# Modulation sums in PSUM banks, closed half a group later

## The chip, the cores and the metric

One core of one Trainium2 chip runs the whole program. The metric is the device time in microseconds (us) of one execution, as a median over several. The engines are PE (TensorE matmul), DVE (VectorE), ACT (ScalarE), POOL (GpSimd) and SP (SyncE, whose queue issues nearly all DMAs here).

## What is computed

A residual stream of 512 tokens by 1024 features, in fp32, goes through two blocks of two layers each. Block 1 has two hybrid layers, each with two attentions and then a squared-relu MLP with 4096 hidden features. Block 2 (an MLA layer and a gated linear attention layer, each with such an MLP) also has a context stream of 256 tokens, and scales and shifts its norms by a modulation vector that does not depend on the tokens:

```python
def modulate(h, shift, scale):
    return h * (1.0 + scale) + shift

def sqrelu_mlp(h, w1, w2):
    return jnp.square(jax.nn.relu(h @ w1)) @ w2
...
    silu_c = jax.nn.silu(c)
    silu_cc = jax.nn.silu(c_ctx)
    for i in range(DEPTH):
        m_lat = (silu_c @ ada_w[i] + ada_b[i]).reshape(B, N_MOD, 1, D)
        m_ctx = (silu_cc @ ada_w[i] + ada_b[i]).reshape(N_MOD, D)
        h_lat = modulate(rms_norm_2(x_lat, norm_g[i, 0]), m_lat[:, 0], m_lat[:, 1])
```

For each layer of block 2 the modulation is thus two vector-matrix products, one for each stream, with the same weight of 1024 by 6144 fp32 (24 MB). The second layer needs only the first 2048 features of the context's vector. These vector-matrix products are what the change is about.

## The kernel before

**Products.** A product of two fp32 operands is made as three products of rounded parts (`mac3`): high by high (L211), low weight by high (L212), high weight by low (L213). Weights come in blocks of 512 KB on the SP queue (L185); ACT rounds them (L190, `wh`), and POOL subtracts to get the remainder (L194, `wl`), reading two SBUF tiles.

**The MLP.** `mlp` runs 8 chunks of 512 hidden features. `first(c+1)` makes 4 groups of 24 matmuls of 512 columns into the PSUM pool `mm` (2 banks), whose results DVE and ACT square and split (L522, L525, L529, L530). `second(c)` makes 8 groups of 12 matmuls, in turn into `mm` and `sp` (pool tag `s`, 4 banks), and DVE adds each to `y` in SBUF (L541). A chunk is 192 matmuls. A third PSUM pool, `tp`, has 2 banks, and serves transposes and small products.

**The modulation in the background.** While the MLP of layer l of block 1 runs, the generator `ada(l)` makes the modulation of layer l of block 2. `mlp` advances it by a step at fixed places: twice ahead of each of the two weight blocks of `first`, and three times (`BG = 3`) ahead of `second`, seven steps a chunk. A group u is 512 of the 6144 features, and takes four steps q. In each step a block `araw` of 2 x 128 rows by 512 features (512 KB, two buffers, SP queue, L1342) is loaded ahead, and DVE multiplies its rows, a row on a partition, with silu(c) of those rows and adds them to an accumulator of 128 partitions by 512, one accumulator for each stream:

```python
if q == 0 and k == 0:
    nc.vector.tensor_scalar(a, raw[:, k], sc, None, op0=ALU.mult)
else:
    nc.vector.scalar_tensor_tensor(a, raw[:, k], sc, a, op0=ALU.mult, op1=ALU.add)
```

That is L1370 and L1372: 16 instructions a group with two streams, 8 with one (layer 1 from u = 4 on). The accumulators (`aacc`) are SBUF tiles, two buffers. The sum over the 128 partitions closes a group, at the start of the first step of the next group: `total` splits an accumulator into a rounded part (ACT, L165) and the rest (DVE, L166) in tiles of the shared pool `tmp`, and PE multiplies both with a column of ones (L1351, L1352) into a bank of `tp`; ACT copies the row (L1354) and SP stores it (L1355).

**Order.** The program is written in this order; a scheduler then orders the instructions of each engine, and each engine runs its own list strictly in order. What an instruction on PE waits for, all matmuls behind it wait for too. The same holds for DVE, on which the accumulations, the splits and the evictions L522 to L541 share one list.

## Time and profile before

| | |
|---|---|
| median of 3 runs | 3557.34 us (3553.0, 3557.34, 3562.2) |
| the profiled execution | span 3557.3 us, nothing outside it that the views show |
| busy, share of the span | PE 93%, PE weight load 80%, DVE 64%, ACT 43%, POOL 33% |
| MLPs with the modulation in the background | from about 450 to 940 us and from about 1390 to 1860 us |
| MLP of the last layer, one stream, nothing in the background | from about 3230 us on |

In the views, PE is the matmul pipeline, "L1352" is line 1352 of the kernel shown above, and an arrow gives what released a wait. A matmul of 512 columns starts every 0.233 us at full clock although its record lasts 0.39 us, since matmuls overlap.

### The profile page before, as it was taken

Reading aid. Unit: us, or ns where it says so; the run is one execution under the profiler, and the core shown is the slowest. Engines: PE = TensorE matmul, PEld = TensorE weight load, DVE = VectorE, ACT = ScalarE, POOL = GpSimd, SP = SyncE. Lnnn points to the kernel's source line nnn. Section 1 sums busy time; section 2 is a strip of 40 time slices with the busy share of each in tenths; the row PEclk is TensorE's granted clock in tenths of the full one; section 3 lists DMA queues with packets and bytes.
Section 4 is the critical chain, followed back from the end, with each engine's and each line's share of the span. In section 5 each row is a group of like instructions: output and inputs, shape, how many; then the busy total and the mean of one; then the engine's idle time right before and its main releaser. Section 6 shows DMA issues by size and latency. Waiting matters only on the chain.

```text
span 3557.3 us, 49004 instructions
## 1 busy us (share of the span) xinstructions
PE 3299.7 (93%) x18723; PEld 2843.9 (80%) x18723; DVE 2263.8 (64%) x4044; ACT 1516.0 (43%) x3323; POOL 1191.2 (33%) x688
## 2 busy tenths in 40 slices
PE   8899988988989998989999999999999899889998
PEld 8788776766878887767778888888888788878887
DVE  6755668887686567886657763723433866873445
ACT  5455543222454454432235654531221456654223
POOL 3333334333333324334431332132232222124443
PEclk8999999999999999999999999999999999999999
DMA  5212444444232235345321113122122212123332
GB/s 171 66 60 75 166 140 152 135 145 131 82 92 72 74 114 177 116 158 176 119 74 59 37 60 97 48 63 68 60 64 63 69 53 66 63 70 95 95 95 77
DMA packets 262097, 337.68 MB, mean 95 GB/s; under 512 B 17107, under 2 KB 178110, under 8 KB 261734
## 3 DMA queue, kind: packets, MB, share of 16 engines
q1 hardware_dynamic: 261862, 334.55, 29.9%
q8 instruction: 147, 2.41, 0.3%
q14 instruction: 88, 0.72, 0.1%
HBM read 305.98 MB, written 28.52 MB: 94 GB/s over the span
## 4 chain that ended last, share of the span: by engine, by line
PE 62%; DVE 22%; ACT 8%; issue 5%; DMA 2%; POOL 1%; SPq 0%; DVEq 0%; ACTq 0%; POOLq 0%
PE mm L211 13%; PE mm L213 13%; PE mm L212 13%; PE s L212 4%; PE s L211 4%; PE s L213 4%; DVE aacc L1372 3%; ACT wh L190 2%; PE s L280 2%; DMA araw<-in_ada_w_dram 2%; DVE t L166 1%; PE tp L1065 1%; DVE t L529 1%; DVE wl L194 1%; PE mm L238 1%
## 5 line engine op out<-in xcount | busy, mean ns | idle before, releaser
L194 POOL TENSOR_TENSOR wl<-wraw,wh 128x1024 fp32r<-128x1024 f32 (+2 forms) x424 | 1008.4, 2397 | 1848.4 <-ACT wh L190 1800.2
L211 PE MATMUL mm<-h,wh 128*128 128x512 f32 (+1 forms) x1916 | 728.4, 380 | 30.1 <-ACT h L1264 8.5
L213 PE MATMUL mm<-h,wh 128*128 128x512 f32 (+1 forms) x1916 | 713.6, 373 | 6.0 <-DVE h L333 3.0
L212 PE MATMUL mm<-h,wl 128*128 128x512 f32 (+1 forms) x1916 | 716.4, 374 | 2.0 <-POOL wl L194 1.6
L190 ACT CAST wh<-wraw 128x1024 fp32r<-128x1024 f32 (+3 forms) x454 | 428.4, 967 | 512.1 <-issue 328.7
L211 PEld LDWEIGHTS mm<-h,wh 128*128 128x128 f32 x1916 | 370.2, 193 | 93.1 <-ACT h L1264 10.3
L213 PEld LDWEIGHTS mm<-h,wh 128*128 128x128 f32 x1916 | 369.1, 193 | 71.6 <-DVE h L1265 4.8
L212 PEld LDWEIGHTS mm<-h,wl 128*128 128x128 f32 x1916 | 371.0, 194 | 54.8 <-POOL wl L194 2.4
L529 DVE TENSOR_TENSOR t<-t 128x512 f32<-128x512 f32 (+1 forms) x140 | 169.2, 1208 | 256.3 <-ACT hid L525 256.0
L1372 DVE SCALAR_TENSOR_TENSOR aacc<-araw,sc,aacc 128x512 f32<-128x512 f32 x280 | 295.3, 1079 | 43.8 <-DMA araw<-in_ada_w_dram 41.8
L211 PE MATMUL mm<-hid,wh 128*128 128x512 f32 (+1 forms) x848 | 294.2, 347 | 9.7 <-DVE y L541 9.7
L212 PE MATMUL mm<-hid,wl 128*128 128x512 f32 (+1 forms) x848 | 292.4, 345 | 0.0
L213 PE MATMUL mm<-hid,wh 128*128 128x512 f32 (+1 forms) x848 | 291.3, 344 | 0.0
L541 DVE TENSOR_TENSOR y<-y,mm 128x512 f32<-128x512 f32 (+1 forms) x192 | 105.4, 549 | 201.7 <-PE mm L213 201.5
L211 PE MATMUL s<-hid,wh 128*128 128x512 f32 (+1 forms) x560 | 211.5, 378 | 0.0
L213 PE MATMUL s<-hid,wh 128*128 128x512 f32 (+1 forms) x560 | 211.4, 377 | 0.0
L212 PE MATMUL s<-hid,wl 128*128 128x512 f32 (+1 forms) x560 | 211.2, 377 | 0.0
L530 DVE TENSOR_TENSOR hid<-t,hid 128x512 fp32r<-128x512 f32 (+1 forms) x176 | 180.5, 1029 | 29.8 <-ACT t L527 25.4
L525 ACT ACTIVATE hid<-t 128x512 fp32r<-128x512 f32 (+1 forms) x176 | 97.2, 554 | 231.3 <-DVE t L522 155.6
L211 PEld LDWEIGHTS mm<-hid,wh 128*128 128x128 f32 x848 | 160.7, 190 | 33.0 <-DVE y L541 6.8
L213 PEld LDWEIGHTS mm<-hid,wh 128*128 128x128 f32 x848 | 160.7, 190 | 21.2
L212 PEld LDWEIGHTS mm<-hid,wl 128*128 128x128 f32 x848 | 160.7, 190 | 21.1 <-issue 0.3
(682 smaller groups left out, 7438.1 us busy)
## 6 DMA issues: line engine op xcount, KB each, us to landing
wraw<-in_w_ff_dram SPq DMA_DIRECT2D x128, 512.0 KB
wraw<-in_mlp_w_dram SPq DMA_DIRECT2D x128, 512.0 KB
araw<-in_ada_w_dram SPq DMA_DIRECT2D x96, 512.0 KB
wraw<-in_w_in_dram SPq DMA_DIRECT2D x68, 512.0 KB
raw<-in_cmp_w_dram SPq DMA_DIRECT2D x16, 512.0 KB
td<-t SPq DMA_DIRECT2D x32, 256.0 KB
h<-td SPq DMA_DIRECT2D x32, 256.0 KB
wraw<-in_w_out_dram SPq DMA_DIRECT2D x16, 512.0 KB
```

Source lines behind the costliest of these rows:

```text
L166: self.nc.vector.tensor_tensor(l, x, h.bitcast(F32), op=ALU.subtract)
L190: i = nc.scalar.copy(h[:, x:z], raw[:, x - a:z - a]).ins
L194: e.tensor_tensor(l[:, x:z], raw[:, x - a:z - a], h[:, x:z].bitcast(F32), op=ALU.subtract)
L211: nc.tensor.matmul(ps, wh, mh, start=first, stop=False)
L212: nc.tensor.matmul(ps, wl, mh, start=False, stop=False)
L213: nc.tensor.matmul(ps, wh, ml, start=False, stop=last)
L280: self.nc.tensor.matmul(ps, self.ones, acc, start=first, stop=last)
L525: nc.scalar.activation(h, a, AF.Square)
L529: nc.vector.tensor_tensor(a, a, a, op=ALU.mult)
L530: nc.vector.tensor_tensor(lo, a, h.bitcast(F32), op=ALU.subtract)
L541: nc.vector.tensor_tensor(y, y, ps, op=ALU.add)
L1372: nc.vector.scalar_tensor_tensor(a, raw[:, k], sc, a, op0=ALU.mult, op1=ALU.add)
```

## The change

The accumulators of `ada` are now PSUM tiles, one bank each, that take both banks of `tp`. The multiply-adds (now L1379 and L1381) read `araw` from SBUF and read and write the bank. A group's split (`part`) still stands at the start of the next group's first step, but goes into tiles of its own, `ada0` and `ada1`, with two buffers each in layer 0 and one in layer 1. For the four groups of layer 1 with two streams there is no split: ACT copies each accumulator in fp32 and one fp32 ones-product takes the copy. The ones-products (now L1363), the row copy (L1365) and the store (L1366) come at the third step of the next group, into a bank of `sp`. A step is added at the end. In `load_ctx` the transposes of the context, which run beside `ada(1)`, take banks of `sp` in place of `tp`. All other lines of the diff only drop comments and docstrings.

```diff
-        def total(u, acc):
-            for s, a in enumerate(acc):
-                h = self.t(self.tmp, [P, 512], F32R, tag="t")
-                lo = self.t(self.tmp, [P, 512], F32R, tag="t")
-                self.split(a, h, lo)
-                ps = self.ps(pool=self.tp, tag="tp")
-                nc.tensor.matmul(ps[0:1], self.onesr[:, 0:1], h, start=True, stop=False)
-                nc.tensor.matmul(ps[0:1], self.onesr[:, 0:1], lo, start=False, stop=True)
+        def part(acc):
+
+            nb = 2 if l == 0 else 1
+            if l and len(acc) == 2:
+                out = [[self.t(pool, [P, 512], F32, tag=f"ada{q}", bufs=nb)] for q in range(2)]
+                for a, (c,) in zip(acc, out):
+                    nc.scalar.copy(c, a)
+                return out
+            out = [[self.t(pool, [P, 512], F32R, tag=f"ada{q}", bufs=nb) for q in range(2)] for _ in acc]
+            for a, hl in zip(acc, out):
+                self.split(a, *hl)
+            return out
+
+        def total(u, parts):
+            for s, ms in enumerate(parts):
+                ps = self.ps(pool=self.sp, tag="s")
+                one = (self.ones if len(ms) == 1 else self.onesr)[:, 0:1]
+                for q, m in enumerate(ms):
+                    nc.tensor.matmul(ps[0:1], one, m, start=q == 0, stop=q == len(ms) - 1)
                 row = self.t(self.tmp, [1, 512], F32, tag="t")
                 nc.scalar.copy(row, ps[0:1])
                 nc.sync.dma_start(md[s, 4 * u:4 * u + 4].rearrange("a p -> (a p)")[None, :], row)
 
         nxt, done = load(0, 0), None
         for u in range(12):
-            if done:
-                total(*done)
-            acc = [self.t(pool, [P, 512], F32, tag="aacc", bufs=2) for _ in range(1 if l == 1 and u >= 4 else 2)]
+            acc = [self.ps(pool=self.tp, tag="tp") for _ in range(1 if l == 1 and u >= 4 else 2)]
             for q in range(4):
                 raw = nxt
                 if (u, q) != (11, 3):
@@ -1370,8 +1379,11 @@
                             nc.vector.tensor_scalar(a, raw[:, k], sc, None, op0=ALU.mult)
                         else:
                             nc.vector.scalar_tensor_tensor(a, raw[:, k], sc, a, op0=ALU.mult, op1=ALU.add)
+                if q == 2 and done:
+                    total(*done)
                 yield
-            done = u, acc
+            done = u, part(acc)
+        yield
         total(*done)
         yield
...
             for k in range(0, KT, 2):
                 if k == 4:
                     xt = load(1)
-                ps = self.ps(pool=self.tp, tag="tp")
+                ps = self.ps(pool=self.sp, tag="s")
                 for kk in range(2):
```

**PE, layer 0, the ones-products that close group u = 4.** Before, the list of PE has them one by one inside groups of `first`: `t_6409` and `t_6410` are the two parts of one stream's sum, `t_6419` and `t_6420` those of the other.

```order
L213 MATMUL mm_6453<-h_4609,wh_6443 128x512
L211 MATMUL mm_6453<-h_4638,wh_6443 128x512
L1351 MATMUL tp_6413<-t_6409,onesr_642 1x512
L212 MATMUL mm_6453<-h_4638,wl_6444 128x512
L213 MATMUL mm_6453<-h_4639,wh_6443 128x512
L211 MATMUL mm_6453<-h_4664,wh_6443 128x512
L1352 MATMUL tp_6413<-t_6410,onesr_642 1x512
L212 MATMUL mm_6453<-h_4664,wl_6444 128x512
L213 MATMUL mm_6453<-h_4665,wh_6443 128x512
```

After, the four stand together between a group of `first` and one of `second` (`ada_6409` and `ada_6410` are the same two parts as before).

```order
L212 MATMUL mm_6471<-h_4740,wl_6432 128x512
L213 MATMUL mm_6471<-h_4741,wh_6431 128x512
L1363 MATMUL s_6507<-ada_1196_6409,onesr_642 1x512
L1363 MATMUL s_6507<-ada_1197_6410,onesr_642 1x512
L1363 MATMUL s_6513<-ada_1198_6411,onesr_642 1x512
L1363 MATMUL s_6513<-ada_1199_6412,onesr_642 1x512
L211 MATMUL mm_6551<-hid_1111_5953,wh_6541 128x512
L212 MATMUL mm_6551<-hid_1111_5953,wl_6542 128x512
```

Each pair has moved from the middle of a group of 24 products to the end of a later one. In the whole list of before, 12 to 30 matmuls stand between the last matmul whose result DVE evicts ahead of a split and the L1352 that takes the split, for 33 of the 40 splits; after the change it is at least 52 for each of the 32 splits.

**DVE, layer 0, the splits of the same group.** Before, the splits L166 stand between the evictions L522 to L530 of `first`, and the first accumulations of the next group go around them.

```order
L522 SCALAR_TENSOR_TENSOR t_6374<-mm_6349,r_94 128x512
L529 TENSOR_TENSOR t_6374<-t_6374 128x512
L530 TENSOR_TENSOR hid_1179_6320<-t_6374,hid_1178_6319 128x512
L522 SCALAR_TENSOR_TENSOR t_6404<-mm_6379,r_94 128x512
L529 TENSOR_TENSOR t_6404<-t_6404 128x512
L166 TENSOR_TENSOR t_6410<-aacc_6173,t_6409 128x512
L530 TENSOR_TENSOR hid_1181_6322<-t_6404,hid_1180_6321 128x512
L1370 TENSOR_SCALAR aacc_6429<-araw_6333,sc_718 128x512
L1372 SCALAR_TENSOR_TENSOR aacc_6429<-araw_6333,sc_718,aacc_6429 128x512
L166 TENSOR_TENSOR t_6420<-aacc_6174,t_6419 128x512
```

After, both stand in a row ahead of that chunk's first L522.

```order
L541 TENSOR_TENSOR y_4754<-y_4754,mm_6279 128x512
L541 TENSOR_TENSOR y_4754<-y_4754,s_6293 128x512
L166 TENSOR_TENSOR ada_1197_6410<-tp_6161,ada_1196_6409 128x512
L166 TENSOR_TENSOR ada_1199_6412<-tp_6162,ada_1198_6411 128x512
L1379 TENSOR_SCALAR tp_6417<-araw_6333,sc_718 128x512
L1379 TENSOR_SCALAR tp_6418<-araw_6333,sc_718 128x512
L1381 SCALAR_TENSOR_TENSOR tp_6417<-araw_6333,sc_718,tp_6417 128x512
L1381 SCALAR_TENSOR_TENSOR tp_6418<-araw_6333,sc_718,tp_6418 128x512
L522 SCALAR_TENSOR_TENSOR t_6374<-mm_6349,r_94 128x512
```

The eviction of `mm_6349` has moved from ahead of both splits to behind them and behind four accumulations.

**DVE, layer 0, the end of the norm ahead of the MLP.** L260 and L287 to L289 end the norm that the MLP's first products need (`acc` and `ry` hold a sum of squares and its inverse root), L299 adds squares, `araw` are blocks of the modulation weight. Before:

```order
L1372 SCALAR_TENSOR_TENSOR aacc_5208<-araw_5236,sc_718,aacc_5208 128x512
L1372 SCALAR_TENSOR_TENSOR aacc_5209<-araw_5236,sc_718,aacc_5209 128x512
L299 TENSOR_TENSOR acc_95<-acc_95,t_4944 128x256
L299 TENSOR_TENSOR acc_95<-acc_95,t_4973 128x256
L299 TENSOR_TENSOR acc_95<-acc_95,t_5002 128x256
L299 TENSOR_TENSOR acc_95<-acc_95,t_5031 128x256
L260 TENSOR_SCALAR acc_95<-s_5093 128x256
L194 TENSOR_TENSOR wl_5223<-wraw_5224,wh_5222 128x512
L287 TENSOR_TENSOR ry_5098<-ry_5092 128x256
```

After:

```order
L1381 SCALAR_TENSOR_TENSOR tp_5603<-araw_5605,sc_718,tp_5603 128x512
L1381 SCALAR_TENSOR_TENSOR tp_5604<-araw_5605,sc_718,tp_5604 128x512
L1381 SCALAR_TENSOR_TENSOR tp_5603<-araw_5605,sc_718,tp_5603 128x512
L299 TENSOR_TENSOR acc_95<-acc_95,t_5031 128x256
L1381 SCALAR_TENSOR_TENSOR tp_5604<-araw_5605,sc_718,tp_5604 128x512
L1381 SCALAR_TENSOR_TENSOR tp_5603<-araw_5611,sc_718,tp_5603 128x512
L1381 SCALAR_TENSOR_TENSOR tp_5604<-araw_5611,sc_718,tp_5604 128x512
L1381 SCALAR_TENSOR_TENSOR tp_5603<-araw_5611,sc_718,tp_5603 128x512
L1381 SCALAR_TENSOR_TENSOR tp_5604<-araw_5611,sc_718,tp_5604 128x512
L1381 SCALAR_TENSOR_TENSOR tp_5603<-araw_5687,sc_718,tp_5603 128x512
L1381 SCALAR_TENSOR_TENSOR tp_5604<-araw_5687,sc_718,tp_5604 128x512
L260 TENSOR_SCALAR acc_95<-s_5093 128x256
```

Ten multiply-adds on three more blocks of weight (`araw_5605`, `araw_5611`, `araw_5687`, of group u = 1) now stand ahead of L260. The start of layer 1 has the same pattern.

## Rows read from the trace of the kernel before

**Rows 1.** The page: the chain that ended last, by line.
```profile
PE mm L211 13%; PE mm L213 13%; PE mm L212 13%; PE s L212 4%; PE s L211 4%; PE s L213 4%; DVE aacc L1372 3%; ACT wh L190 2%; PE s L280 2%; DMA araw<-in_ada_w_dram 2%; DVE t L166 1%; PE tp L1065 1%; DVE t L529 1%; DVE wl L194 1%; PE mm L238 1%
```

**Rows 2.** Windows of five chunks: stretch, length, busy PE, PEld, DVE, ACT, POOL, clock, DMA, GB/s.
```profile
623.00:900.00 277.00, 247.32 (x1012) 192.68 (x1013) 226.41 (x257) 71.22 (x95) 103.62 (x40) 0.94 0.43 133
1552.00:1817.00 265.00, 241.08 (x994) 190.89 (x995) 177.73 (x198) 65.65 (x87) 102.17 (x40) 0.95 0.44 139
3279.00:3500.00 221.00, 221.00 (x961) 180.06 (x960) 89.69 (x81) 62.32 (x80) 99.83 (x41) 1.00 0.31 96
```

**Rows 3.** PE's waits, MLP of layer 0 (450 to 940): total us, times, longest.
```profile
PE tp L1352 <- DVE t L166: 38.7, 13, 6.3
PE tp L1351 <- ACT t L165: 5.5, 4, 3.6
```

**Rows 4.** PE's waits, MLP of layer 1 (1390 to 1860).
```profile
PE tp L1352 <- DVE t L166: 27.4, 11, 3.6
PE tp L1351 <- ACT t L165: 4.8, 3, 3.2
```

**Rows 5.** PE's waits in the five chunks 623 to 900 alone.
```profile
PE tp L1352 <- DVE t L166: 27.0, 8, 4.5
PE tp L1351 <- ACT t L165: 3.6, 1, 3.6
PE mm L211 <- DVE t L522: 2.2, 1, 2.2
```

**Rows 6.** PE's waits in the five chunks 1552 to 1817 alone.
```profile
PE tp L1352 <- DVE t L166: 21.8, 6, 3.6
PE tp L1351 <- ACT t L165: 3.2, 1, 3.2
PE mm L211 <- DVE t L522: 2.5, 1, 2.5
```

**Rows 7.** Timeline of PE, layer 1: start, duration, instruction, [idle before it].
```profile
1708.23 0.39 PE L213 MATMUL mm<-hid,wh 128*128 128x512 f32 x1
1708.46 0.40 PE L211 MATMUL s<-hid,wh 128*128 128x512 f32 x1
1712.50 0.39 PE L1352 MATMUL tp<-t,onesr 128*1 128x512 f32 x1 [3.64 <-DVE t L166]
...
1714.38 0.63 PE L211 MATMUL s<-hid,wh 128*128 128x512 f32 x1
1714.81 0.63 PE L212 MATMUL s<-hid,wl 128*128 128x512 f32 x1
```

**Rows 8.** DVE's groups, whole run: busy us, mean ns, idle us before and its cause.
```profile
L1372 DVE SCALAR_TENSOR_TENSOR aacc<-araw,sc,aacc 128x512 f32<-128x512 f32 x280 | 295.3, 1079 | 43.8 <-DMA araw<-in_ada_w_dram 41.8
L166 DVE TENSOR_TENSOR t<-aacc,t 128x512 fp32r<-128x512 f32 x40 | 57.9, 1448 | 11.0 <-ACT t L165 10.9
```

**Rows 9.** Instructions of tile aacc and of line 541: shortest/median/longest ns.
```profile
L1372 DVE SCALAR_TENSOR_TENSOR aacc<-araw,sc,aacc x280: 736/747/2907, 456.0 to 1740.8; 128x512 f32<-128x512 f32 x140
...
L541 DVE TENSOR_TENSOR y<-y,mm x192: 404/547/690, 623.9 to 3547.9; 128x512 f32<-128x512 f32 x96, 128x256 f32<-128x256 f32 x96
```

**Rows 10.** DVE's groups between 600 and 900.
```profile
L1372 DVE SCALAR_TENSOR_TENSOR aacc<-araw,sc,aacc 128x512 f32<-128x512 f32 x120 | 127.3, 1088 | 7.5 <-DMA araw<-in_ada_w_dram 7.0
```

**Rows 11.** The chain between 560 and 575: start, duration, what.
```profile
570.13 3.84 DMA araw<-in_ada_w_dram
```

**Rows 12.** Timeline of PE, layer 0: fp32 ones-products of 256 columns, and what follows.
```profile
487.60 0.59 PE L280 MATMUL s<-acc,ones 128*128 128x256 f32 x2
...
488.15 0.28 PE L212 MATMUL mm<-h,wl 128*128 128x256 f32 x1
```

**Rows 13.** Timelines of DVE and of the SP queue, start of the MLP of layer 0.
```profile
468.67 0.75 DVE L1372 SCALAR_TENSOR_TENSOR aacc<-araw,sc,aacc 128x512 f32<-128x512 f32 x1 [8.62 <-DMA araw<-in_ada_w_dram]
...
479.40 0.37 SPq L1342 DMA_DIRECT2D araw<-in_ada_w_dram  x1
...
488.85 0.43 DVE L260 TENSOR_SCALAR acc<-s 128x256 f32<-128x256 f32 x1 [5.70 <-ACT ry L146]
```

## The prediction

> **What bounds the kernel now.** PE first. In the by-line chain the matmul lines L211 to L213 lead, but the accumulation L1372 holds 3% of it and the arrival of `araw` 2% [rows 1]. So the background work, which should cost PE only its ones-products, decides the end in places. How much it costs is best read by windows, since the MLP of the last layer does the same five chunks without it: 221.0 us there, with PE never idle and a granted clock of 1.00; 277.0 us in layer 0 and 265.0 us in layer 1, with the clock at 0.94 and 0.95 [rows 2]. The excess is 56.0 + 44.0 = 100.0 us for ten chunks of the sixteen.
>
> The list of PE's waits says where this sits. PE waits at L1352 for the split's second part and at L1351 for its first: 38.7 + 5.5 us in layer 0, 27.4 + 4.8 us in layer 1, **76.4 us** in all [rows 3, 4]. Within the ten chunks it is 27.0 + 3.6 + 21.8 + 3.2 = 55.6 us, and another 2.2 + 2.5 = 4.7 us are waits of L211 for an eviction [rows 5, 6].
>
> The timeline of PE shows one such wait: 3.64 us idle ahead of L1352. Ahead of it matmuls start 0.23 us apart; a little behind it they start 0.43 us apart [rows 7]. [...]
>
> The account of the ten chunks closes. Five chunks are 35 steps or 8.75 groups: 17.5 splits in layer 0 and, mostly with one stream, some 9.5 in layer 1. Two ones-products for each are 54 x 0.233 = 12.6 us. Then 100.0 - 55.6 - 4.7 - 12.6 = **27.1 us** are left for the clock; the clock column alone gives (1 - 0.94) x 277 + (1 - 0.95) x 265 = 29.9 us, which also counts time in which PE stood idle [rows 2]. I use 25.
>
> Why is the split late? It shares DVE's list with the accumulations, and DVE is busy 226.4 of 277 us [rows 2]. An accumulation takes 1.08 us on average and a split 1.45 us [rows 8]. Yet undisturbed the accumulation takes 0.75 us (its median), and its longest takes 2.91 us, while the eviction L541 of the same size, with one operand in PSUM, never exceeds 0.69 us [rows 9]. POOL is busy about 100 us of each window with remainders that read two SBUF tiles [rows 2]. So instructions with two SBUF operands are stretched beside POOL, and those with a PSUM operand are not.
>
> **The change part by part.**
>
> *The distance of the ones-products.* The four now stand at least 52 matmuls behind the work that frees the split, in place of mostly 12 to 30. The longest wait seen is 6.3 us [rows 3]; ahead of it 15 matmuls or 3.5 us had passed, so 9.8 us would have been enough, and 52 matmuls are 12.1 us. All 76.4 us of waits go. Bounds: at most these, and at least half, if the waits move elsewhere on PE (rival B).
>
> *The clock.* With the waits goes the slow stretch behind each: 25 us, bounds 13 and 30. In the chunks outside the two windows I count none, as the norm at the layer's start keeps interrupting PE there.
>
> *The accumulators in PSUM.* No row shows DVE writing a PSUM tile. The nearest is L541, which reads one and takes 0.69 us [rows 9]; the other end is 1.45 us, the stretched split [rows 8]. I take 0.69, since the change leaves one SBUF operand, as L541 has. Between 600 and 900 us that takes 120 x (1.09 - 0.69) = 48 us off DVE [rows 10], and the splits shrink too, so DVE falls from 82% to under 65% of the old length. This is not on the path by itself; what it buys is that DVE follows when a chunk takes 45.8 us (44.2 from 221.0 / 5, plus 7 ones-products) in place of 55.4.
>
> The longest of L541 against the shortest of L1372 (0.69 against 0.74 us [rows 9]) shows no surcharge for a PSUM operand. [...]
>
> *The fp32 ones-products.* In layer 1's first four groups eight fp32 products replace sixteen rounded ones. Two fp32 products' worth of 256 columns and one 0.12 us matmul fill 487.60 to 488.15 [rows 12], thus 0.43 us for 256 columns and 0.85 us for 512, against 2 x 0.233: 8 x 0.38 = **+3 us**, bounds 2 and 4.
>
> *The start of each layer.* Ten accumulations on three more blocks now stand ahead of L260, on which the norm and then the first products wait. Before, L260 started at 488.85 us when ACT was ready, and the first of these blocks was issued at 479.40 [rows 13]. A block lands 3.84 us after its issue where the chain shows it [rows 11], at 483.2; its four accumulations end at 486.0; the third block needs its buffer, lands at 489.9 at best, and two accumulations later it is 491.3: 2.4 us late. The queue is shared with weights, and here DVE has waited 8.62 us for one block [rows 13], nearly 5 us above the best case. Halfway, 5 us, plus the accumulation in front of L287 and a stretch of slow clock: 7 us a layer, **+14 us** for both. Bounds: 0, if ACT's part also comes late, and 25.
>
> *New waits.* The splits stand ahead of `mm`'s eviction in DVE's list, and wait for ACT's rounding. L1372's 41.8 us of waits for `araw` [rows 8] may grow, since a faster DVE sooner stands at a block not yet landed. PE's cover is two banks of `mm`. I let the 4.7 us of eviction waits double: **+5 us**, bounds 0 and 40. The later store, the context's transposes in other banks, and the added step cost nothing: the first product that needs the modulation comes after the whole MLP, and `sp` has four banks.
>
> *Sum:* -76.4 - 25 + 3 + 14 + 5 = -79.4 us. The profiled span, 3557.3 us, is the median of the runs, so the forecast is **3478 us**.
>
> **The rivals.**
>
> *B, the wait moves to the evictions.* Three steps taken in a row are twelve accumulations, 8.3 us at 0.69, and one block's arrival of 3.84 us, 12.1 us in all. If L541 queues behind all of them, PE's cover is three groups of 12 products, 8.4 us, and 3.7 us of wait stay in each of about ten chunks with two streams; with the clock behind each wait, another 0.8 us apiece, that is 45 us. Less the 5 already in the sum, the time is about 3518 us. Against it: the same burst took 17 us before and PE waited 2.2 us for evictions in five chunks [rows 5]. For it: PE was then held back at L1352 anyway, which gave DVE time.
>
> *C, the waits only change their names.* If each split makes DVE wait for ACT behind weight roundings, `mm`'s eviction is late by what L1352 waited for, and nothing is won: about 3550 us. Against it: DVE waited 10.9 us at 40 splits [rows 8], 0.3 us each.
>
> *D, slower: PSUM accumulations are slow.* A multiply-add that reads and writes the same bank, one behind another, might not run at L541's rate. In layer 0 DVE has 226.4 - 127.3 = 99 us of other work in five chunks [rows 2, 10], 19.8 a chunk, so at d us each a chunk takes 19.8 + 24d and DVE becomes the bound of the old 55.4 us at d = 1.48. Layer 1, with half the accumulations, still wins about 38 us; from d = 1.7 on, seven chunks of layer 0 lose more than that. At 2.0 us it is 7 x 12.4 - 38 = +49 us, about 3606 us.
>
> **How the numbers follow.** My forecast has a chance of 0.72, with its own range 3445 (no cost at the starts, the clock at its upper bound, waits outside the windows with their clock too) to 3500. B has 0.18, C 0.06, D 0.04. The range 3440 to 3523 holds the forecast's case and most of B. A difference of 0.3%, 10.7 us, is about what a measurement of this kernel tells from no change. The forecast's case and B are faster by more (0.90), C is the same (0.06), D slower (0.04).
>
> **What would show it.** In the new trace PE's waits at L1363 should be near 0 us, the granted clock in the MLP chunks 0.98 or more, five chunks in the middle of layer 0 about 230 us long, L1381 about 0.69 us with no long tail, and L260 at the start of each layer some microseconds behind ACT, with `araw` as the reason. Waits of L211 for L522 or L541 above 10 us per layer would mean B; splits waiting for ACT by microseconds, C; L1381 above 1.5 us, D. The prediction is wrong if the starts of the layers cost more than 25 us, or if DVE, though faster, comes later to the evictions than before.

## Result and the profile after

The changed kernel takes 3444.03 us in the median of 4 runs (3442.27 to 3449.81), against 3559.35 us for the kernel before. The ratio is 0.9684, with a 95% interval of 0.967 to 0.9697. That is 115 us less, where the forecast was 79 us less (3478 us): the mechanism came as foretold, and the gain was nearly half as large again. The time lies inside the wide range of the prediction (3440 to 3523 us) and 1 us below the range of the forecast's own case (3445 to 3500 us).

The windows of the same five chunks as in [rows 2], from the first eviction of a chunk to that of the fifth after it, with the same columns:

```profile
602.40:834.90 232.50, 232.50 (x1010) 185.03 (x1009) 178.22 (x246) 68.21 (x94) 101.17 (x41) 1.00 0.51 159
1475.80:1703.90 228.10, 227.96 (x985) 181.80 (x984) 149.28 (x185) 62.93 (x84) 101.72 (x41) 1.00 0.49 155
```

Layer 0's chunks take 232.5 us in place of 277.0, layer 1's 228.1 in place of 265.0, and the granted clock is 1.00 where it was 0.94 and 0.95. PE is without a pause; what is left above the 221.0 us of the last layer is mostly the ones-products themselves. The same stretches in the trace of the kernel before, between the same evictions ([rows 2] has round limits):

```profile
623.80:900.40 276.60, 246.98 (x1012) 192.38 (x1011) 226.01 (x255) 70.90 (x95) 103.62 (x40) 0.94 0.43 134
1552.90:1817.50 264.60, 240.76 (x994) 190.57 (x993) 177.33 (x196) 65.26 (x87) 102.21 (x40) 0.95 0.44 140
```

PE's largest waits in the MLP of layer 0, which answer to [rows 3]:

```profile
PE mm L211 <- ACT h L332: 4.8, 2, 4.1
PE mm L211 <- ACT h L1264: 4.2, 2, 3.4
PE mm L211 <- DVE y L541: 3.4, 2, 2.2
```

No ones-product (L1363) is among the waits, and no L522, which stood in [rows 5] and [rows 6]. The by-line chain, which answers to [rows 1], has lost L1372 and L166, and `araw` is down to 1%:

```profile
PE mm L211 15%; PE mm L213 15%; PE mm L212 15%; PE s L212 4%; PE s L211 4%; PE s L213 4%; PE s L280 2%; ACT wh L190 1%; DMA araw<-in_ada_w_dram 1%; POOL wl L194 1%; PE tp L1065 1%; PE mm L238 1%; PE mm L239 1%; PE mm L240 1%; DVE y L308 1%
```

The accumulations, by the shortest, median and longest time of an instruction (as [rows 9]), and DVE's groups in the five chunks of layer 0 (as [rows 10]):

```profile
L1381 DVE SCALAR_TENSOR_TENSOR tp<-araw,sc,tp x280: 740/751/759, 454.4 to 1624.6; 128x512 f32<-128x512 f32 x140
...
L1379 DVE TENSOR_SCALAR tp<-araw,sc x40: 739/746/755, 453.1 to 1615.2; 128x512 f32<-128x512 f32 x40
```

```profile
L1381 DVE SCALAR_TENSOR_TENSOR tp<-araw,sc,tp 128x512 f32<-128x512 f32 x104 | 74.9, 750 | 9.8 <-DMA araw<-in_ada_w_dram 9.5
L530 DVE TENSOR_TENSOR hid<-t,hid 128x512 fp32r<-128x512 f32 x21 | 27.0, 1286 | 0.3
L529 DVE TENSOR_TENSOR t<-t 128x512 f32<-128x512 f32 x21 | 26.1, 1244 | 8.5 <-ACT hid L525 8.4
...
L166 DVE TENSOR_TENSOR ada<-tp,ada 128x512 fp32r<-128x512 f32 x16 | 10.3, 683 | 5.1 <-ACT ada L165 5.1
```

The accumulation's tail is gone: from 736/747/2907 ns to 740/751/759. But it is not as quick as L541 (at most 0.69 us [rows 9]), and the two instructions of the eviction whose two operands both lie in SBUF, L529 (which reads one tile twice) and L530, take 1.24 and 1.29 us here. In the same chunks before they took 1.12 and 0.69:

```profile
L1372 DVE SCALAR_TENSOR_TENSOR aacc<-araw,sc,aacc 128x512 f32<-128x512 f32 x112 | 119.6, 1093 | 7.5 <-DMA araw<-in_ada_w_dram 7.0
L166 DVE TENSOR_TENSOR t<-aacc,t 128x512 fp32r<-128x512 f32 x17 | 23.6, 1389 | 3.5 <-ACT t L165 3.5
L529 DVE TENSOR_TENSOR t<-t 128x512 f32<-128x512 f32 x20 | 22.4, 1120 | 10.0 <-ACT hid L525 9.9
...
L530 DVE TENSOR_TENSOR hid<-t,hid 128x512 fp32r<-128x512 f32 x20 | 13.7, 686 | 0.3
```

The stretch has moved on to them.

### The profile page after: what moved, and what is told of

Same layout as the page of the kernel before. It is cut to its first block, busy times and chain, and to the rows that moved or that the text cites. A ratio compares the mean times of both kernels' runs of the same rounds, so it can differ in the third digit from the quotient of the medians.

```text
span 3442.1 us, 48999 instructions
## 1 busy us (share of the span) xinstructions
PE 3267.2 (95%) x18723; PEld 2826.3 (82%) x18723; DVE 2147.2 (62%) x4036; ACT 1512.3 (44%) x3323; POOL 1174.1 (34%) x688
## 4 chain that ended last, share of the span: by engine, by line
PE 69%; DVE 16%; ACT 7%; issue 4%; DMA 2%; POOL 1%; SPq 0%; DVEq 0%; ACTq 0%; POOLq 0%
PE mm L211 15%; PE mm L213 15%; PE mm L212 15%; PE s L212 4%; PE s L211 4%; PE s L213 4%; PE s L280 2%; ACT wh L190 1%; DMA araw<-in_ada_w_dram 1%; POOL wl L194 1%; PE tp L1065 1%; PE mm L238 1%; PE mm L239 1%; PE mm L240 1%; DVE y L308 1%
## 5 line engine op out<-in xcount | busy, mean ns | idle before, releaser
L194 POOL TENSOR_TENSOR wl<-wraw,wh 128x1024 fp32r<-128x1024 f32 (+2 forms) x424 | 993.3, 2361 | 1750.8 <-ACT wh L190 1703.2
L529 DVE TENSOR_TENSOR t<-t 128x512 f32<-128x512 f32 (+1 forms) x140 | 173.1, 1237 | 255.2 <-ACT hid L525 255.1
L1381 DVE SCALAR_TENSOR_TENSOR tp<-araw,sc,tp 128x512 f32<-128x512 f32 x280 | 200.7, 751 | 57.6 <-DMA araw<-in_ada_w_dram 56.2
L541 DVE TENSOR_TENSOR y<-y,mm 128x512 f32<-128x512 f32 (+1 forms) x192 | 105.4, 549 | 196.4 <-PE mm L213 196.4
L530 DVE TENSOR_TENSOR hid<-t,hid 128x512 fp32r<-128x512 f32 (+1 forms) x176 | 199.5, 1138 | 29.0 <-ACT t L527 24.3
L213 PEld LDWEIGHTS mm<-hid,wh 128*128 128x128 f32 x848 | 159.2, 188 | 20.9
```

The costliest lines, as they stand in the source:

```text
L194: e.tensor_tensor(l[:, x:z], raw[:, x - a:z - a], h[:, x:z].bitcast(F32), op=ALU.subtract)
L213: nc.tensor.matmul(ps, wh, ml, start=False, stop=last)
L529: nc.vector.tensor_tensor(a, a, a, op=ALU.mult)
L530: nc.vector.tensor_tensor(lo, a, h.bitcast(F32), op=ALU.subtract)
L541: nc.vector.tensor_tensor(y, y, ps, op=ALU.add)
```

## Experiments

Each ran beside the kernel before on the same chip; ratios are to it. "Five chunks" are those of layer 0, read as above.

```
run                     median us   ratio (95%)              five chunks us
before                  3559.35                              276.6
changed                 3444.03     0.9684 (0.967 0.9697)    232.5
e1_late_sbuf            3533.24     0.993  (0.9915 0.9945)   256.3
e2b_psum_only           3489.55     0.9808 (0.9791 0.9824)   255.6
e2_psum_early           3441.05     0.9674 (0.966 0.9688)    232.3
e3b_behind_norm         3447.96     0.9694 (0.9679 0.9708)   229.8
e5_fp32                 3463.21     0.9736 (0.9722 0.9751)   240.4
e6_noread_before        3429.19     0.9639 (0.9625 0.9653)   230.7
e6_noread_late          3435.19     0.9657 (0.9641 0.9673)   229.2
e6_noread_after         3435.68     0.9657 (0.9643 0.9671)   230.6
e9_writes_before        3440.74     0.9672 (0.9659 0.9685)   233.8
e7_halves_before        3477.62     0.9781 (0.9765 0.9797)   265.7
e7_halves_e2            3405.71     0.9571 (0.9557 0.9585)   232.2
e8_quarters_e2          3384.87     0.9511 (0.9497 0.9525)   232.0
```

**Each part alone.** First the later ones-products without PSUM sums, in layer 0 alone. Against the changed kernel:

```diff
-            acc = [self.ps(pool=self.tp, tag="tp") for _ in range(1 if l == 1 and u >= 4 else 2)]
+            if done and l:
+                early(*done)
+            acc = [self.t(pool, [P, 512], F32, tag="aacc", bufs=2) for _ in range(1 if l == 1 and u >= 4 else 2)]
...
-                if q == 2 and done:
+                if q == 2 and done and l == 0:
                     total(*done)
```

(`early` is `total` of the kernel before.)

> Layer 0 alone is changed: the sums stay in SBUF, but their parts go into tiles of their own and the ones-products come at the third step of the next group (at least 54 matmuls behind, as in the changed kernel); layer 1 is as before. Theory 1 (the distance of the ones-products is what removes PE's waits, and DVE's speed only has to suffice): layer 0's waits at the ones-products (44.2 us) and the slow clock behind them go, some waits for evictions come in their place because accumulations still take 1.08 us; five chunks of layer 0 take 235 to 245 us in place of 276.6, and the run 3505 to 3520 us. Theory 2 (DVE's speed, won by the PSUM operand, is what removes the waits): DVE is as busy as before, so the waits move to the evictions, five chunks take 260 us or more, and the run 3540 us or more.

The run gained 23 us (0.993), between the two theories. PE's waits in the five chunks are now these:

```profile
PE mm L211 <- DVE t L522: 11.0, 4, 3.7
PE mm L211 <- DVE y L541: 6.3, 3, 5.6
```

The waits at the ones-products are gone, and 17.3 us of waits for evictions have come in their place, where 2.2 us stood [rows 5]: rival B of the prediction, which a DVE still at 1.06 us an accumulation brings about.

Then the sums in PSUM without the rest:

```diff
-            acc = [self.t(pool, [P, 512], F32, tag="aacc", bufs=2) for _ in range(1 if l == 1 and u >= 4 else 2)]
+            acc = [self.ps(pool=self.tp, tag="tp") for _ in range(1 if l == 1 and u >= 4 else 2)]
...
-                ps = self.ps(pool=self.tp, tag="tp")
+                ps = self.ps(pool=self.sp, tag="s")
```

> The sums in PSUM banks alone: parts go into the shared tiles as before, and the ones-products come right behind, 12 to 30 matmuls after the work that frees the split, as before (into banks of sp). Theory 1 (distance): DVE reaches the split sooner since accumulations take 0.75 us, so of the 76.4 us of waits about half stay, 30 to 45 us, with slow clock behind them: 3490 to 3510 us. Theory 2 (DVE's speed): waits below 15 us, and 3465 us or less.

3489.6 us: 0.4 us below the first theory's range, far from the second's. 20.9 + 6.7 us of waits stay in layer 0 and 11.2 + 5.6 in layer 1, 44.4 in place of 76.4. In the five chunks of layer 0, DVE's groups:

```profile
L1372 DVE SCALAR_TENSOR_TENSOR tp<-araw,sc,tp 128x512 f32<-128x512 f32 x112 | 79.8, 749 | 8.1 <-DMA araw<-in_ada_w_dram 7.6
L530 DVE TENSOR_TENSOR hid<-t,hid 128x512 fp32r<-128x512 f32 x20 | 29.9, 1495 | 0.3
L529 DVE TENSOR_TENSOR t<-t 128x512 f32<-128x512 f32 x20 | 26.2, 1309 | 10.3 <-ACT hid L525 10.3
```

The accumulations run at 0.75 us, but L530, which stands between an eviction and the split, takes 1.50 us where it took 0.69. So of layer 0's 44.1 us, the distance alone gave 20.3 (276.6 to 256.3) and the speed alone 21.0 (to 255.6): they nearly add up (41.3 us), and neither is enough by itself.

**The place in the program.** The split from tiles of its own, but the ones-products written right behind it:

```diff
         for u in range(12):
+            if done:
+                total(*done)
             acc = [self.ps(pool=self.tp, tag="tp") for _ in range(1 if l == 1 and u >= 4 else 2)]
...
-                if q == 2 and done:
-                    total(*done)
                 yield
```

> The changed kernel, with the ones-products written at the old place of the program, right behind the split, but still from tiles of their own. In the list of PE they come out 54 to 204 matmuls behind all the same. Theory 1 (the tiles of their own give the distance, not the place in the program): as the changed kernel, 3444 us within 8, no wait at the ones-products. Rival (the later place in the program is needed): waits at the ones-products of 30 us and more, and 3480 us or more.

3441.05 us, not to be told from the changed kernel. Idle time ahead of the ones-products is 0.0 us (the number behind the second bar):

```profile
L1363 PE MATMUL s<-ada,onesr 128*1 128x512 f32 x64 | 18.2, 396 | 0.0
...
L1363 PE MATMUL s<-ada,ones 128*1 128x512 f32 x16 | 7.5, 591 | 0.0
```

"Half a group later" in the source does nothing. This run and the one with PSUM sums alone differ in the tiles of the parts (and in layer 1's fp32 copies). What moves the ones-products is thus that their operands are no longer tiles of the shared pool, with four buffers that every eviction needs: then the scheduler is free to put them 54 to 204 matmuls behind, wherever they are written.

**The start of the layers.** No accumulation ahead of the norm:

```diff
-                if bg is not None:
+                if bg is not None and c:
                     next(bg, None)
...
-                            nc.vector.tensor_scalar(a, raw[:, k], sc, None, op0=ALU.mult)
+                            i = nc.vector.tensor_scalar(a, raw[:, k], sc, None, op0=ALU.mult).ins
+                            if u == 0:
+                                self.tc.add_manual_dep(i, self.normed.name, NOSYNC, reason="order")
```

> The changed kernel, but no step of the background work ahead of the first chunk, and the first accumulation of a layer is ordered behind the L260 that ends the norm of the second half of the tokens: no accumulation stands ahead of the norm that the first products wait for. If the accumulations in front of L260 cost what PE waits for there (two waits of L211 for L332, 4.8 us in layer 0 and 4.6 us in layer 1): 8 us less, about 3436 us. If the start costs nothing, 3444 us within 3. If the background work, now begun some 50 us later, does not end in time with the MLP: 3455 us or more.

3447.96 us, not faster. The waits at L332 are all but gone (0.2 us in each layer), and those at L280 have grown from 2.5 and 5.3 us to these, in layer 0 and in layer 1:

```profile
PE s L280 <- ACT y L322: 5.6, 4, 2.7
```

```profile
PE s L280 <- ACT y L322: 7.1, 4, 2.7
```

The norm does get through sooner without the accumulations, however. L260 takes the result of an L280 that sums `acc`; here are both at the start of layer 0, from the timelines of PE and DVE, in the changed kernel and then in this run:

```profile
483.17 0.59 PE L280 MATMUL s<-acc,ones 128*128 128x256 f32 x2
486.10 1.42 DVE L1381 SCALAR_TENSOR_TENSOR tp<-araw,sc,tp 128x512 f32<-128x512 f32 x2 [1.03 <-DMA araw<-in_ada_w_dram]
487.43 0.42 DVE L260 TENSOR_SCALAR acc<-s 128x256 f32<-128x256 f32 x1
493.58 0.58 PE L211 MATMUL mm<-h,wh 128*128 128x256 f32 x1 [4.07 <-ACT h L332]
```

```profile
484.02 0.59 PE L280 MATMUL s<-acc,ones 128*128 128x256 f32 x2
485.28 0.42 DVE L260 TENSOR_SCALAR acc<-s 128x256 f32<-128x256 f32 x1 [5.70 <-ACT ry L146]
```

In the changed kernel L260 starts 4.26 us behind L280, here 1.26, and before 1.25 us (487.60 and 488.85 [rows 12, 13]). So it is 3.0 us late behind the third block's first two accumulations, near the 2.4 that the prediction had as the best case. What of this reaches PE is the time from that L280 to the first product of 512 columns, with which the next chunk begins:

```
us from L280 to the next chunk    before                       changed                      e3b_behind_norm
layer 0                           531.13 - 487.60 = 43.53      528.83 - 483.17 = 45.66      527.72 - 484.02 = 43.70
layer 1                           1455.38 - 1411.67 = 43.71    1389.90 - 1344.39 = 45.51    1387.69 - 1343.98 = 43.71
```

The hoisted accumulations cost PE 2.1 us in layer 0 and 1.8 us in layer 1, and their absence gives that back. The run loses it again behind the norm: in layer 1 the next chunk begins 2.2 us sooner than in the changed kernel, but the first L541 comes 4.0 us later (1479.8 us against 1475.8), with 2.9 us of waits for L522 in that layer, where the changed kernel has none. That the accumulations, begun later, crowd there is likely and was not tested. The total of this run therefore doesn't tell what the start costs; the table does.

**The price of an fp32 ones-product.** Every sum in fp32:

```diff
-            if l and len(acc) == 2:
-                out = [[self.t(pool, [P, 512], F32, tag=f"ada{q}", bufs=nb)] for q in range(2)]
+            if True:
+                out = [[self.t(pool, [P, 512], F32, tag=f"ada{q}", bufs=nb)] for q in range(len(acc))]
```

> The changed kernel, with an fp32 copy by ACT and one fp32 ones-product for every sum, in place of a split and two rounded products for 32 of the 40. Two fp32 products took 1.81 us and two pairs of rounded ones 0.93 us, so 32 sums cost 32 x 0.44 = 14 us more of PE, and DVE loses 32 splits or 22 us. If PE alone sets the pace now: 3456 to 3460 us. If DVE still holds PE up in places: 3448 us or less.

19 us more than the changed kernel, above the 14 forecast, and five chunks 240.4 us in place of 232.5: DVE was relieved of 32 splits, and nothing came of it: PE sets the pace. Of the 19, 3.1 us stand ahead of any ones-product: the L280 of layer 0's norm comes at 486.24 us in place of 483.17, in a stretch that the edit leaves alone. So two runs can differ by that much there, and some 2 us are left open. In the changed kernel two fp32 products (four records) and what follows them start at

```profile
1400.90 1.88 PE L1363 MATMUL s<-ada,ones 128*1 128x512 f32 x4
1402.71 0.50 PE L211 MATMUL mm<-h,wh 128*128 128x512 f32 x1
```

1.81 us apart; so for the eight of layer 1 the change pays 8 x (0.90 - 0.47) = 3.5 us, near the forecast's 3.

**What stretches DVE.** POOL's reads taken away, in the kernel before:

```diff
-                    e.tensor_tensor(l[:, x:z], raw[:, x - a:z - a], h[:, x:z].bitcast(F32), op=ALU.subtract)
+                    if e is nc.gpsimd and self.bare:
+                        nc.gpsimd.memset(l[:, x:z].bitcast(F32), 0.0)
+                    else:
+                        e.tensor_tensor(l[:, x:z], raw[:, x - a:z - a], h[:, x:z].bitcast(F32), op=ALU.subtract)
```

(`bare` is set during the MLPs with the modulation in the background.)

> The kernel before, but in block 1's MLPs POOL fills the low parts of the weights with zeros instead of subtracting (it writes them and reads no SBUF tile; so the products with the low parts are of zeros). Sums stay in SBUF, ones-products stay close behind. Theory (the accumulations are stretched by POOL's reads of SBUF): L1372 falls from 1.08 to 0.75 us and the splits to 0.69 us, PE's waits at the ones-products fall to about 45 us as with PSUM sums alone, 3480 to 3505 us. Rival (the stretch comes from something else in SBUF, and only PSUM cures it): L1372 stays above 1.0 us, and 3545 us or more.

3429.19 us: faster than the changed kernel, with neither part of the change in it. The same five chunks, DVE's groups and PE's only waits:

```profile
L1378 DVE SCALAR_TENSOR_TENSOR aacc<-araw,sc,aacc 128x512 f32<-128x512 f32 x112 | 80.6, 747 | 12.6 <-DMA araw<-in_ada_w_dram 12.1
L533 DVE TENSOR_TENSOR t<-t 128x512 f32<-128x512 f32 x20 | 13.8, 691 | 10.6 <-ACT hid L529 10.4
...
L534 DVE TENSOR_TENSOR hid<-t,hid 128x512 fp32r<-128x512 f32 x20 | 13.8, 688 | 0.3
...
L167 DVE TENSOR_TENSOR t<-aacc,t 128x512 fp32r<-128x512 f32 x17 | 11.7, 687 | 2.6 <-ACT t L166 2.6
```

```profile
PE tp L1357 <- ACT t L166: 0.4, 1, 0.4
PE tp L1358 <- DVE t L167: 0.3, 1, 0.3
```

All four run at their undisturbed 0.69 or 0.75 us, and the ones-products, as close behind the splits as in the kernel before, make PE wait 0.7 us in all. I had expected some 45 us of waits to stay, as with PSUM sums alone. What the traces show to differ between the two runs on DVE is L529 and L530, which PSUM sums leave exposed and which POOL then stretches all the more (1.31 and 1.50 us against 0.69).

A control, with POOL as busy as before but only writing (`for v in (1.0, 0.5, 0.0)` around the same fill):

> The kernel before, with POOL filling the low parts of the weights of block 1's MLPs three times over (the last time with zeros, so the products with the low parts are of zeros): about 2.9 us of POOL for a block in place of 2.5, all writes, no read of SBUF. Theory (POOL's reads stretch DVE's instructions with two SBUF operands, and nothing else of POOL does): as with one filling, L1372 about 0.80 us, no wait at the ones-products, 3425 to 3440 us. Rival (that POOL is busy, or its writes, or low parts that come late): L1372 above 1.0 us, waits at the ones-products above 40 us, 3510 us or more.

```profile
L1379 DVE SCALAR_TENSOR_TENSOR aacc<-araw,sc,aacc 128x512 f32<-128x512 f32 x112 | 80.5, 746 | 12.3 <-DMA araw<-in_ada_w_dram 11.7
L1377 DVE TENSOR_SCALAR aacc<-araw,sc 128x512 f32<-128x512 f32 x16 | 12.8, 797 | 1.0 <-DMA araw<-in_ada_w_dram 0.9
```

```profile
603.00:836.80 233.80, 229.87 (x992) 180.34 (x991) 162.75 (x255) 69.99 (x94) 109.22 (x119) 1.00 0.51 157
```

POOL is busy for 109.2 us in these chunks, more than the 103.6 of [rows 2], and the accumulation still takes 0.75 us; 9.9 us of waits at L1359 are left in both layers, and 3440.74 us. The other three instructions with two SBUF operands take 692, 688 and 685 ns in these chunks (L529, L530 and the split L166 of the kernel before, there 1120, 686 and 1389 ns). For an instruction of this kind it is POOL's reads, not that POOL works, nor its writes. The plain multiply L1377 (L1370 before), from one SBUF tile into another, behaves otherwise: in this run it takes 0.80 us on average in these chunks, and 0.48 in the run with a single filling (e6_noread_before, at most 0.49). On POOL the two runs differ in the added fills alone, so POOL's writes do stretch an instruction of that kind.

The same fill in the kernel with layer 0's later ones-products, and in the changed kernel:

> The same zeros from POOL, with layer 0's ones-products later and from tiles of their own; sums in SBUF in both layers, layer 1 otherwise as before. If PSUM sums matter only because they escape POOL's reads, layer 0 is as fast as in the changed kernel (five chunks 228 to 236 us) and layer 1 as in the run without the later products: 3465 to 3480 us. If the PSUM bank gives something more, layer 0's five chunks stay above 240 us.

> The changed kernel with the same zeros from POOL, as a control for what the zeros change by themselves. PE already runs without a pause in the chunks, so nothing is won there: 3444 us within 6. If low parts that come earlier also help, 3435 us or less.

3435.19 us and 3435.68: five chunks take 229.2 and 230.6 us. The first was expected 30 us slower, on the view that close ones-products in layer 1 would still wait; they do not. The control gained 8 us, a little more than allowed for. Without POOL's reads the three arrangements stand within 6.5 us, and the kernel before is the lowest of them, at the edge of what the intervals separate.

**POOL's instructions in pieces.** If DVE waits for whole instructions of POOL, shorter ones should help, with nothing left out. Halves, in the kernel before and in the one of the early place:

```diff
-                    e.tensor_tensor(l[:, x:z], raw[:, x - a:z - a], h[:, x:z].bitcast(F32), op=ALU.subtract)
+                    m = (x + z) // 2 if e is nc.gpsimd and z - x > 1 else z
+                    for p, q in ((x, m), (m, z)):
+                        if p < q:
+                            e.tensor_tensor(l[:, p:q], raw[:, p - a:q - a], h[:, p:q].bitcast(F32), op=ALU.subtract)
```

The trace of the kernel before shows such a wait, on POOL and then on DVE:

```profile
742.11 4.96 POOL L194 TENSOR_TENSOR wl<-wraw,wh 128x1024 fp32r<-128x1024 f32 x2 [5.95 <-ACT wh L190]
```

```profile
744.84 2.78 DVE L1372 SCALAR_TENSOR_TENSOR aacc<-araw,sc,aacc 128x512 f32<-128x512 f32 x1
```

POOL's second subtraction ends at 747.07 us, and the accumulation, which started inside it, at 747.62, 0.55 us later. All 51 accumulations of that run that took over 0.81 us started inside an instruction of POOL with two SBUF operands (48 times such a subtraction, 3 times an addition L299) and ended 0.55 us behind its end (0.547 to 0.560 us), however long it still had to run.

> The kernel before, with each of POOL's subtractions done as two of half the size; nothing is left out. If a DVE instruction that meets one of POOL's waits for its end, the longest L1372 falls from 2.9 to about 2.2 us, and with shorter worst cases PE's waits at the ones-products fall from 76 to 40 to 60 us: 3505 to 3540 us. If both engines share the reads evenly, the mean of L1372 and the time stay: 3550 to 3565 us.

> The same two halves in the changed kernel with the ones-products written at the old place (the fastest complete kernel so far, 3441 us). In block 1's MLP chunks PE has no wait left to win, but halves may help the attention stages and the starts of the layers, where DVE's instructions with two SBUF operands stand on the path: 3425 to 3438 us if they do, 3441 us within 4 if not, 3448 us or more if POOL's extra instructions cost PE waits for low parts.

The longest accumulation in the first of them, beside 2907 ns in [rows 9]:

```profile
L1375 DVE SCALAR_TENSOR_TENSOR aacc<-araw,sc,aacc x280: 733/751/1839, 443.6 to 1687.2; 128x512 f32<-128x512 f32 x140
```

In this run 99 accumulations took over 0.81 us, and they too end 0.54 to 0.55 us behind the end of POOL's instruction, a half in 95 cases. 3477.62 us, 80 us less, more than expected; 50.1 + 15.2 = 65.3 us of waits at its ones-products stay, of 76.4 before, so most of the gain is elsewhere. In the second, 3405.71 us, the place is clear: layer 0's first eviction of a chunk comes 9.5 us earlier than without halves, layer 1's 25.5 and the last layer's 34.6 us, while the five chunks keep their length (232.3 and 232.2 us). The gain lies ahead of the MLPs and between them, where the attentions are; which of their instructions gained is not shown.

> As with the halves, in the same kernel, but POOL's subtractions now one row block at a time: 256 columns for the first weight of an MLP and the projections with 256 features (four in place of one), 512 for the rest. If a DVE instruction is held for at most one POOL instruction, the stretch shrinks further where the pieces are 256 columns: the means of the two-operand instructions of the MLP fall below 0.95 us, and the run gains again, 3390 to 3402 us. But 256 columns took 0.92 us of POOL against 1.38 for 512 and 2.5 for 1024, so POOL gets slower by a third; if low parts then come late, PE waits for them and the run is 3406 us or more.

3384.87 us, better than expected, although POOL is busy 1361.1 us in place of 1174.1. Most of POOL's pieces and DVE's instruction that gains most:

```profile
L197 POOL TENSOR_TENSOR wl<-wraw,wh 128x256 fp32r<-128x256 f32 x966 | 728.5, 791 | 944.5 <-ACT wh L190 857.5 <-issue 83.2 <-DVE x L312 3.4
```

```profile
L533 DVE TENSOR_TENSOR hid<-t,hid 128x256 fp32r<-128x256 f32 x64 | 40.2, 630 | 26.2 <-ACT t L530 24.9
```

L533 here is L530 of the kernel before, 1.03 us in the changed kernel in this shape. The condition named for a gain, two-operand means below 0.95 us, holds for it and not for the 512-column ones (0.953 and 0.970). This version beats both kernels, the one before by 4.9% and the changed one by 1.7% (3384.87 / 3444.03).

## Why the prediction was right, and where it was not

*The waits* went as worked out: those at the ones-products are gone, 76.4 us, and the chunks' clock is back at 1.00. Ten chunks are 44.1 + 36.5 = 80.6 us shorter (276.6 to 232.5 and 264.6 to 228.1, between exact evictions).

*The clock* was set too low at 25 us. In the prediction's account the waits of the ten chunks are read too high: PE stood idle for 277.00 - 247.32 = 29.7 and 265.00 - 241.08 = 23.9 us there [rows 2], while the waits listed add up to 32.8 and 27.5 us [rows 5, 6], because a wait that reaches into the window is listed whole. With 53.6 us of idle time in place of 60.3, the remainder for the clock is 33.8 and not 27.1 us. And the chunks outside the two windows count as well. Over all the chunks of both MLPs behind the norm, from the same product to the same product, PE's busy time falls from 342.15 + 343.33 to 325.40 + 330.98 us, in the kernel before and in the changed one:

```profile
523.50:912.20 388.70, 342.15 (x1444) 267.49 (x1444) 313.70 (x351) 108.34 (x150) 150.62 (x58) 0.95 0.43 135
1445.30:1825.90 380.60, 343.33 (x1462) 270.94 (x1461) 266.46 (x298) 110.35 (x162) 147.12 (x57) 0.96 0.44 140
```

```profile
521.10:846.50 325.40, 325.40 (x1445) 260.96 (x1445) 241.92 (x333) 104.28 (x148) 143.00 (x58) 1.00 0.50 154
1379.90:1711.90 332.00, 330.98 (x1463) 262.41 (x1461) 215.51 (x274) 107.28 (x158) 141.42 (x58) 1.00 0.48 154
```

That is 29.1 us although the fp32 products cost 3.5 us more, so the clock gave some 32 us.

*The PSUM accumulations* have no tail, as said; their time is 0.75 us, not 0.69. DVE is busy 178 us, 64% of the old length, as forecast ("under 65%"), but partly by luck: accumulations and splits fell by 58 us in the five chunks of layer 0 (119.6 + 23.6 to 74.9 + 10.3), eight accumulations fewer falling into them, and L529 and L530, which the prediction left as they were, took 17 us of it back (22.4 + 13.7 to 26.1 + 27.0).

*The terms that failed are "the start of each layer", +14 us, and "new waits", +5 us.* Of the first the mechanism is right: the hoisted accumulations make L260 late, and the first products with it. But what reaches PE is 2.1 + 1.8 = 3.9 us (the table of the run e3b_behind_norm). The prediction raised 2.4 us to 7 because DVE had once waited 8.62 us for a block; the last of the blocks ahead of L260 was waited for 1.03 us in layer 0 and 1.35 in layer 1. The second had the wrong sign: with quicker accumulations and splits the 7.2 us at L522 in the two MLPs (2.2 and 5.0) went, instead of doubling.

With these the account of the 115 us closes, by the profiled executions. The forecast missed 36 us of them: 10 at the starts, 12 at the new waits, 7 at the clock, and some 7 in stretches that the change doesn't touch (4.4 ahead of layer 0's norm, where the L280 came at 487.60 and 483.17 us, the rest between and behind the MLPs). Why those differ is open; the run of e5 differs from the changed kernel by 3.1 us in the first of them, which its edit leaves alone. All four misses have the same sign, so none hid another.

*The reason given for late splits was right in kind and too narrow in extent.* The prediction looked at accumulations and splits beside POOL. In fact the eviction's L529 and L530 are hit as well when they start inside a subtraction (1.24 and 1.29 us on average in the changed kernel's five chunks, 0.69 without POOL's reads), and what is freed in one place is taken at another. So "distance" and "speed" are two covers for one cause: with POOL's reads gone, neither is needed (3429.19 us in e6_noread_before). And the reading of the order was right about the distance, but the distance is due to the tiles, not to the half group.

*The rivals.* B came true exactly where DVE stayed slow and only the distance was changed (17.3 us of eviction waits in e1). No run shows the 0.8 us of clock with which B reckons behind each wait: in the trace of the kernel before, the granted clock is 0.50 from 1713.4 to 1716.4 us, behind the wait of [rows 7], and from 1713.20 to 1716.85 nine matmuls start 0.33 to 0.43 us apart, 1.55 us more in all than at 0.233. C and D did not come: DVE waits 7.9 us in all for ACT at the splits, and no accumulation takes over 0.76 us.

The accumulation in SBUF takes 0.75 us on average with POOL only writing (e9_writes_before), against 1.09 us with POOL reading [rows 10]. A PSUM operand makes neither the accumulation nor an addition or subtraction dearer: 751 ns in the bank (the changed kernel's median) against 747 in SBUF (the median of e6_noread_before), and for two tiles added or subtracted 683 ns with one in PSUM against 687 ns with both in SBUF (in the five chunks of e6_noread_before).

## What to carry to other kernels

When a small operation makes PE wait, first ask why its producer is late. Compare the median with the longest of the producer's instructions: a tail as long as another engine's instruction suggests that the two engines collide (here 2.91 us beside subtractions of 2.5 us), and a look at which operands stretch tells where. A cure at the source (shorter POOL instructions) can be worth more than moving the consumer (80 us with halves alone in e7_halves_before, 23 us with layer 0's later ones-products alone in e1_late_sbuf), and it also helps stages at which nobody was looking (halves brought the first eviction of layer 1's MLP 25.5 us forward).

Tiles from a pool that everything shares tie an operation to its place in the list; tiles of its own let the scheduler move it, wherever it is written.

## What the runs showed of the hardware

- A multiply-add on DVE that reads and writes a PSUM bank (128 x 512, fp32, one operand from SBUF) takes 751 ns at the median (changed kernel), like 747 ns in SBUF without POOL's reads (e6_noread_before). The plain multiply loses: 746 ns into PSUM against 481 ns into SBUF, at the median of the same two runs.
- A multiply-add on DVE with two SBUF operands that was stretched had started inside an instruction of POOL with two SBUF operands, and ended 0.55 us behind that instruction's end: 51 of 51 before, 99 of 99 with halves (e7_halves_before), of those over 0.81 us. So it waits for the rest of one instruction, and no longer: the longest was 2907 ns beside subtractions of 2.5 us, and 1839 ns beside those of 1.4 us.
- POOL's writes leave such an instruction alone (746 ns in e9_writes_before), but stretch the plain multiply from SBUF into SBUF (797 ns on average there, against 482 ns in e6_noread_before). Into PSUM that multiply takes 739 to 755 ns in the changed kernel, where POOL reads.
- POOL's subtraction of 128 x 256 takes 0.79 us and 128 x 512 1.44 us (e8_quarters_e2), 128 x 1024 2.5 us (before), so quarters cost POOL more time in all (1361.1 us in place of 1174.1), and the kernel was still faster with them (3384.87 us in place of 3444.03).
